# One accumulation of 512 columns instead of two of 256 in the input projection

## The chip, the cores and the metric

The kernel runs on one core of one Trainium2 chip. A core has five engines with an instruction queue each: TensorE (PE in the profile, with its weight loads as PEld), VectorE (DVE), ScalarE (ACT), GpSimd (POOL) and SyncE (SP, which here issues the DMAs). The metric is the device time of one execution in microseconds, median of three runs.

## The reference

Two layers of a mixer. Each layer modulates and normalises 256 context tokens and 2048 latent tokens of width 1024, multiplies them by one input projection, feeds a gated short convolution and a gated DeltaNet scan that runs in both directions, and multiplies the joined outputs by an output projection.

```python
pl = split_proj(to_scan_order(hl, col_major) @ w_in)
pc = split_proj(hc @ w_in)
dl = deltanet_inputs(pl[4], pl[5], pl[6], pl[8], pl[9], conv_qkv, a_log, dt_bias, seg_l)
dc = deltanet_inputs(pc[4], pc[5], pc[6], pc[8], pc[9], conv_qkv, a_log, dt_bias, seg_c)
ol, oc = bidirectional_gdn(dl, dc, ctx_out)
yl = from_scan_order(branch_outputs(pl, ol, conv_a, gdn_norm, seg_l), col_major)
xl = xl + gate_l * (yl @ w_out)
```

The scan solves a triangular system for every tile of tokens and then goes from tile to tile with a 128 by 128 state: `u = u0 - w s`, `s_new = s * decay + k u`.

## The kernel before

**Tokens and channels.** The 18 tiles of 128 tokens are cut into five chunks: chunk 0 is the context (256 tokens), chunks 1 to 4 are 512 latent tokens each. Activations lie channel-major in a high and a low part (`h` and `l`; `hc` and `lc` for the context). A unit is 128 output channels of `w_in`, whose weights are split in the same way (`whi`, `wlo`). `project` makes one unit of one chunk: 8 blocks of 128 input channels, three products each, so 24 passes over a chunk. `phase` walks over units and chunks and hands each result to a consumer (`conv`, tanh, multiply, store) that reads all columns of the accumulator at once.

**How many.** Per layer there are 32 units and four chunks of 512 tokens: 128 projections, 256 in both layers.

**The scan.** `delta` handles one head: for 16 tiles it transposes q, k, v (L495) and makes the k-k and q-k products (L511). Then comes one solve for all 16 tiles: multiplications and transposes on DVE (L543, L552), a transfer through DRAM that regroups blocks, a loop of 31 steps on DVE (L573, L575), a transfer back, and groups of small matmuls (L601, L610, L612, L630, L631, L637, L638) with DVE work between them (L582 to L640). Only then come the 32 scan steps of the head (two directions, 16 tiles). The chain of a step is L684 (PE), L686 (DVE), L689 (PE), L692 (DVE), L694 (PE), L703 (DVE), and then L684 of the next tile. L712 and L713 make the output of a step; `finish` turns finished tiles (L661, L662).

**The order.** The program is written with priorities (`urgent` raises them), and a list scheduler with a timeline of its own fixes the order of instructions on each engine when the kernel is built. Each engine then works its list strictly in that order. In layer 0 and layer 1 the scans of the four heads are emitted beside the last projections (`phase` with chunks 3 and 4 and later units), so small matmuls of the scan stand between projection matmuls. The output projection (L899, 512 columns) needs the finished tiles of all four heads.

Of the kernel before, what the change touches and what calls it, by code (L numbers as in the profile page):

```python
# [14 lines left out]
DRAM = bass.MemoryType.DRAM  # L15
# [14 lines left out]
CW = 256  # L30
# [6 lines left out]
def hybrid_backbone_kernel(ctx_stack: ExitStack, tc: tile.TileContext,  # L37
# [26 lines left out]
    turn = [0]  # L64

    def pidle():
        """The scan's banks in turn, for phases without a scan."""
        turn[0] += 1
        return pscan(("c0", "c1", "o")[turn[0] % 3])

# [32 lines left out]
            nc.vector.tensor_copy(csil[:, :, r:r + 1], ps[:, 8 * r:8 * r + 8].unsqueeze(2))  # L103

    def vectors(l, P):
        """Per-channel vectors of the layer, one column each."""
        rows = dp.tile([88, 128], F32, tag="dm", bufs=3, name="rows")
        nc.sync.dma_start(out=rows[0:24], in_=b_mod[l].rearrange("(k p) -> k p", p=128))
        nc.sync.dma_start(out=rows[24:32], in_=norm_w[l].rearrange("(k p) -> k p", p=128))
        nc.sync.dma_start(out=rows[32:44], in_=conv_a[l].rearrange("j (k p) -> (j k) p", p=128))  # L110
        nc.sync.dma_start(out=rows[44:80], in_=conv_qkv[l].rearrange("j (k p) -> (j k) p", p=128))
        nc.sync.dma_start(out=rows[80:81], in_=gdn_norm[l:l + 1])
        ps = pt()
        nc.tensor.transpose(ps[:, 0:81], rows[0:81], ident[0:81, 0:81])
        par = lp.tile([128, 88], F32, tag=f"par{l}", name="par")
        nc.vector.tensor_copy(par[:, 0:44], ps[:, 0:44])
        nc.vector.tensor_copy(par[:, 44:80], ps[:, 44:80])
        nc.vector.tensor_scalar(par[:, 32:44], par[:, 32:44], 0.5, None, ALU.mult)
        nc.vector.tensor_scalar(par[:, 80:81], ps[:, 80:81], 0.5, None, ALU.mult)
        P["par"] = par  # L120
        ab = lp.tile([128, 16], F32, tag=f"ab{l}", name="ab")
        nc.sync.dma_start(out=ab[:, 0:8], in_=a_log[l].rearrange("d h -> (d h)").partition_broadcast(128))
        nc.sync.dma_start(out=ab[:, 8:16], in_=dt_bias[l].rearrange("d h -> (d h)").partition_broadcast(128))
        nc.scalar.activation(ab[:, 0:8], ab[:, 0:8], AF.Exp)
        P["ab"] = ab
        P["mod"] = lp.tile([128, 24, 2], F32, tag=f"mod{l}", name="mod")
# [2 lines left out]
        nc.sync.dma_start(out=wm, in_=w_mod[l][:, 128 * j0:128 * j0 + 128 * n].rearrange("(k p) c -> p k c", p=128))  # L129

    def mod_piece(l, P, wm, j0, n, small):
        """Modulation of the n channel tiles from j0 on, for both kinds of tokens."""
        W = 128 * n
        acc = pd()
        for r in range(2):
            for q in range(4):
                k = 4 * r + q
                nc.tensor.matmul(acc[32 * q:32 * q + 32, 0:W], csil[:, k, :], wm[:, k, :], start=(r == 0), stop=(r == 1))
        acs = cp.tile([128, 512], F32, tag="y", bufs=YB, name="acs")
        nc.vector.tensor_copy(acs[:, 0:W], acc[:, 0:W])  # L140
        ps2 = small()
        for j in range(n):
            nc.tensor.matmul(ps2[:, 2 * j:2 * j + 2], acs[:, 128 * j:128 * j + 128], sel[:, 0:2], start=True, stop=True)
        nc.vector.tensor_tensor(P["mod"][:, j0:j0 + n, :], ps2[:, 0:2 * n].rearrange("p (j r) -> p j r", r=2),
                                P["par"][:, j0:j0 + n].unsqueeze(2).to_broadcast([128, n, 2]), ALU.add)
# [23 lines left out]
        nc.sync.dma_start(out=t, in_=cx[128 * g:128 * g + 128] if g < 2 else lat[128 * (g - 2):128 * (g - 2) + 128])  # L169

    def store_tokens(l, g, t):
        """Layer 0 writes its tokens in the scan order of layer 1, layer 1 in the order of the output."""
        if g < 2:
            nc.sync.dma_start(out=xc1[128 * g:128 * g + 128], in_=t)
            return
        n = GW if l == 0 else GR
        v = x1.rearrange("(w r) d -> r w d", r=GR) if l == 0 else out[0].rearrange("(r w) d -> w r d", w=GW)
        for q in range(128 // n):
            nc.sync.dma_start(out=v[(128 // n) * (g - 2) + q], in_=t[n * q:n * q + n])
# [12 lines left out]
        return dp.tile(shape, F32, tag="m2", bufs=4, name="hf")  # L192

    def prep_load(l, g0, n, tags):
        """Normalised tokens of the n tiles from g0 on. tags: the kinds of buffers they lie in, two tiles to each u but one to u.1."""
        xs = []
        for tag in tags:
            if tag[0] == "u":
# [14 lines left out]
        return xs  # L213

    def prep(P, xs, n, r, hi, lo, bank, bw, acc, keep):
        """Modulate n tiles of normalised tokens, channel-major, split them in two parts, and project on bw into acc. keep: where they are kept in DRAM."""
        for i in range(0, n, 2):
            o = slice(128 * i, 128 * i + 256)
            for k2 in range(0, KT, 2):
# [52 lines left out]
    def project(w, h):  # L272
        W = h[0].shape[-1]
        acc = pd()[:, 0:W]
        passes = [(k, i, j) for k in range(KT) for i, j in ((0, 0), (0, 1), (1, 0))]
        for c in range(0, W, CW):
            for z, (k, i, j) in enumerate(passes):
                nc.tensor.matmul(acc[:, c:c + CW], w[i][:, k, :], h[j][:, k, c:c + CW], start=(z == 0), stop=(z == len(passes) - 1))  # L278
        return acc

    def conv(dst, src, w, segs):
        """dst = segment convolution of src, w the three per-channel weights."""
        nc.scalar.activation(dst, src, AF.Identity, scale=w[1])
        n = dst.shape[-1]
        d3 = dst.rearrange("p (s t) -> p s t", t=segs)
# [2 lines left out]
        nc.vector.scalar_tensor_tensor(d3[:, :, 0:segs - 1], s3[:, :, 1:segs], w[2], d3[:, :, 0:segs - 1], ALU.mult, ALU.add)  # L288

    def layer(l, nxt):  # L290
        """Emits layer l; yields where the layer before it may go on. nxt: the layer after it."""
        ctx_out = l < LAYERS - 1
        seg_l = GW if l == 0 else GR
        P = {}
# [22 lines left out]
        bw = ba_weights()  # L317

        def logits(acc, ci, small, z_):
            """Sum the parts in acc: the write gate of the chunk, and its decay logits into z_."""  # L320
            g0, n = CHUNKS[ci]
            W = 128 * n
            part = stage([128, 512], n)
# [9 lines left out]
            return cp.tile([128, 8, 8], F32, tag=nm, bufs=1, name=nm)  # L333

        def gates(g0, n, z_, small):
            """Write gates and decays of the n tiles from g0 on."""
            gs = slice(g0, g0 + n)
            sm = lambda nm: small_tile(nm)[:, 0:n, :]
            bt = beta[:, gs, :]
# [36 lines left out]
            nc.sync.dma_start(out=row_d[8 * g0:8 * g0 + f8], in_=rw[0:f8])  # L376

        def qkv_unit(s, h):
            """s: 0 q, 1 k, 2 v."""
            par = P["par"]  # L380
            cw = [par[:, 44 + 12 * j + 4 * s + h:45 + 12 * j + 4 * s + h] for j in range(3)]

# [54 lines left out]
            return [unit(u) for u in (0, 2, 1, 3)]  # L437

        def phase(units, pairs, hs, after=None, again=False, ready={}):
            """units: (first column, consumer); the first and last two units go pair by pair."""  # L440
            N = len(units)
            tasks = []
            i = 0
# [30 lines left out]
        states = {}  # L474

        def delta(items, with_out, first):
            """items: (head, tile) pairs; each head's tiles are scanned both ways. Yields before the second eight."""
            n = len(items)
            U = []
            ssk = dp.tile([128, 16], F32, tag="ssk", bufs=2, name="ssk")  # L480
# [165 lines left out]
            og = {}  # L646

            def finish(h, i, o2):
                """Both directions are in o2: normalise two tiles, turn them channel-major."""
                g = items[i][1]  # L650
                tp = pscan("o")
                oT = dp.tile([128, 256], F32, tag="oT", bufs=1, name="oT")
# [97 lines left out]
        hs = {}  # L750

        def prep_pairs(ps, early={}, bank=pidle):
            """Operands and gates of the pairs ps."""
            g0, n = CHUNKS[ps[0]][0], sum(CHUNKS[p][1] for p in ps)
            with urgent():
                z_ = small_tile("g_z")
# [97 lines left out]
        mixes = [0]  # L854

        def mixed(g, aside):
            """Operands of tile g. aside: they leave the weights' buffers alone."""
            t0 = 128 * g
            ys = [dp.tile([128, 4, 128], F32, tag="m2", bufs=4, name="ys") for _ in range(2)]
            for i, yr in enumerate(ys):  # L860
# [96 lines left out]
```

## Time and profile before

| | |
|---|---|
| three runs | 2876.04, 2879.31, 2884.07 us |
| span of the profiled execution, first to last instruction | 2868.8 us |
| PE busy, share of the span | 96% |
| DVE busy | 63% |
| mean granted TensorE clock | 0.982 |

The profile gives the span of the profiled execution; its own time outside the span is not recorded apart, and the timed runs are 7.2 to 15.3 us longer than this span (the median 10.5 us). A busy PE is not a PE at its peak, because matmuls overlap: what counts is the distance from the start of one matmul to the start of the next.

### The profile page before, as it was taken

How to read it: one execution, taken by the hardware profiler on the slowest of the kernel's cores; microseconds unless marked ns; L12 is line 12 of the kernel's file. 1: busy time of each engine (PE TensorE's matmuls, PEld its weight loads, DVE VectorE, ACT ScalarE, POOL GpSimd, SP SyncE). 2: the span in 40 equal slices, each digit the busy share in tenths (PEclk: the TensorE clock that was granted, in tenths of full speed). 3: DMA queues.
4: the chain of work that ended last, by engine and by line, in shares of the span. 5: the costliest groups of instructions: out<-in, count | busy, mean ns of one | idle time of the engine just before them, and what ended most of it. 6: DMA issues, size and time to landing. Idle time of an engine off the chain costs nothing. (4 is left out here: it accounts for less than half of the span.)

```text
span 2868.8 us, 62580 instructions
## 1 busy us (share of the span) xinstructions
PE 2740.4 (96%) x23671; PEld 2529.1 (88%) x23671; DVE 1794.5 (63%) x4677; ACT 1139.6 (40%) x2962; POOL 1002.2 (35%) x1354
## 2 busy tenths in 40 slices
PE   7999999999999999999999999999999998999998
PEld 5799899988988999997777998899999888899887
DVE  5686657576586585353246776675766765754765
ACT  3544453533534532232115444435335354322332
POOL 2332322333433343234444222313334333333443
PEclk9999999999999999999999999999999999999999
DMA  8844265553655553347757552545546556434654
GB/s 275 251 120 138 81 174 130 174 162 89 182 145 170 173 139 113 109 149 246 239 161 242 162 144 79 154 112 163 154 115 188 132 168 189 126 116 118 206 173 117
DMA packets 589449, 450.17 MB, mean 157 GB/s; under 512 B 105322, under 2 KB 527196, under 8 KB 589148
## 3 DMA queue, kind: packets, MB, share of 16 engines
q1 hardware_dynamic: 589148, 446.16, 53.7%
q8 instruction: 188, 3.08, 0.4%
q14 instruction: 113, 0.93, 0.1%
HBM read 326.35 MB, written 119.70 MB: 155 GB/s over the span
## 5 line engine op out<-in xcount | busy, mean ns | idle before, releaser
L278 PE MATMUL pd<-h,whi 128*128 128x256 f32 x4096 | 1206.6, 295 | 2.1 <-ACT whi L251 2.1
L278 PE MATMUL pd<-l,whi 128*128 128x256 f32 x4096 | 1207.2, 295 | 0.0
L278 PE MATMUL pd<-h,wlo 128*128 128x256 f32 x4096 | 1199.4, 293 | 0.5 <-POOL wlo L253 0.5
L278 PEld LDWEIGHTS pd<-h,whi 128*128 128x128 f32 x4096 | 795.2, 194 | 11.9 <-issue 6.6
L278 PEld LDWEIGHTS pd<-l,whi 128*128 128x128 f32 x4096 | 795.0, 194 | 9.0 <-issue 5.4
L278 PEld LDWEIGHTS pd<-h,wlo 128*128 128x128 f32 x4096 | 794.8, 194 | 6.4 <-issue 2.9
L253 POOL TENSOR_TENSOR wlo<-raw,whi 128x1024 fp32r<-128x1024 f32 (+1 forms) x148 | 341.3, 2307 | 382.3 <-ACT whi L251 349.7
L899 PE MATMUL pd<-who,yy 128*128 128x512 f32 x1088 | 350.7, 397 | 0.4 <-ACT who L841 0.4
L899 PEld LDWEIGHTS pd<-who,yy 128*128 128x128 f32 x1088 | 203.6, 189 | 48.0 <-ACT yy L874 2.9
L697 ACT ACTIVATE w<-pscan,cs 128x128 f32<-128x128 f32 x272 | 99.5, 367 | 291.8 <-DVE wk L692 209.1
L899 PE MATMUL pd<-wlo,yy 128*128 128x512 f32 x544 | 214.1, 393 | 0.0
L251 ACT CAST whi<-raw 128x1024 fp32r<-128x1024 f32 x148 | 154.7, 1045 | 97.4 <-PE pd L278 60.9
L501 POOL TENSOR_TENSOR nk<-nk,phalf 128x1 f32<-128x1 f32 x144 | 81.7, 567 | 225.2 <-DVE nk L500 205.8
L573 DVE TENSOR_TENSOR tmp<-L,X 64x31 f32<-64x31 f32 (+15 forms) x310 | 127.1, 410 | 39.9 <-DMA L<-blk 25.0
L388 ACT ACTIVATE pd<-y 128x512 f32<-128x512 f32 (+1 forms) x116 | 65.5, 565 | 213.0 <-DVE y L288 200.6
L686 DVE SCALAR_TENSOR_TENSOR r<-pscan,eg,rc 128x128 f32<-128x128 f32 x272 | 93.7, 346 | 76.7 <-PE pscan L684 74.5
L575 DVE TENSOR_TENSOR X<-X,tmp 64x31 f32<-64x31 f32 (+15 forms) x310 | 136.3, 440 | 5.6
L692 DVE TENSOR_SCALAR wk<-pscan,cs 128x128 f32<-128x128 f32 x272 | 93.5, 346 | 69.6 <-PE pscan L689 67.7
L875 POOL TENSOR_TENSOR yy<-ys,yy 128x512 fp32r<-128x512 f32 x68 | 89.9, 1323 | 125.4 <-ACT yy L874 118.3
L660 POOL TENSOR_TENSOR so<-so,mhalf 128x1 f32<-128x1 f32 x136 | 79.2, 590 | 142.5 <-DVE so L659 134.3
L703 DVE SCALAR_TENSOR_TENSOR Sn<-Sn,atot,pscan 128x128 f32<-128x128 f32 x240 | 82.0, 342 | 67.9 <-PE pscan L694 66.6
L874 ACT CAST yy<-ys 128x512 fp32r<-128x512 f32 x68 | 42.1, 619 | 198.2 <-DVE ys L867 136.8
(2212 smaller groups left out, 5317.3 us busy)
## 6 DMA issues: line engine op xcount, KB each, us to landing
raw<-in_w_in_dram SPq DMA_DIRECT2D x148, 512.0 KB, 4.8
rc<-rec_d SPq DMA_DIRECT2D x272, 256.0 KB, 3.1
rec<-rec_d SPq DMA_DIRECT2D x136, 192.0 KB, 2.6
wm<-in_w_mod_dram SPq DMA_DIRECT2D x24, 1024.0 KB, 7.3
rec_d<-y SPq DMA_DIRECT2D x96, 256.0 KB, 2.9
rows<-row_d SPq DMA_DIRECT2D x144, 128.0 KB, 4.1
rec_d<-rec SPq DMA_DIRECT2D x144, 128.0 KB, 4.0
ys<-y_d SPq DMA_DIRECT2D x68, 256.0 KB, 3.5
```

The costliest lines, as they stand in the source:

```text
L251: nc.scalar.copy(hi, raw)
L253: eng.tensor_sub(lo[:, k], raw[:, k], hi[:, k].bitcast(F32))
L278: nc.tensor.matmul(acc[:, c:c + CW], w[i][:, k, :], h[j][:, k, c:c + CW], start=(z == 0), stop=(z == len(passes) - 1))
L501: nc.gpsimd.tensor_tensor(nk[:, i:i + 1], nk[:, i:i + 1], phalf[:, 0:1], ALU.pow)
L573: nc.vector.tensor_tensor(t3, L3[:, j + 1:32, j:j + 1].to_broadcast([2 * nb, m, k]), X3[:, j:j + 1, 0:k].to_broadcast([2 * nb, m, k]), ALU ...
L575: nc.vector.tensor_sub(X3[:, j + 1:32, 0:k], X3[:, j + 1:32, 0:k], t3)
L686: nc.vector.scalar_tensor_tensor(r, p1[:, 0:128], eg[:, g, col], vn, ALU.mult, ALU.subtract)
L692: nc.vector.tensor_scalar(wk, p2[:, 0:128], cs[:, 5 + z0 + d, i:i + 1], None, ALU.mult)
L697: nc.scalar.activation(w, p2[:, 0:128], AF.Copy, scale=cs[:, z0 + d, i:i + 1])
L703: nc.vector.scalar_tensor_tensor(Sn, S, atot[:, g, col], p3[:, 0:128], ALU.mult, ALU.add)
L875: nc.gpsimd.tensor_sub(l_, yr, h_.bitcast(F32))
L899: nc.tensor.matmul(acc, yy[k // 4][:, k % 4, :], wo[k][part][:, cs_], start=(z == 0), stop=(z == 23))
```

## The change

`project` loses the loop over halves of 256 columns. A chunk of 512 tokens is now accumulated in 24 matmuls of 512 columns; before, it took 48 of 256 columns, first all 24 for the left half, then all 24 for the right half. Columns and products are the same; every weight block is loaded once where it was loaded twice. The context chunk (256 columns) stays as it was.

```diff
         acc = pd()[:, 0:W]
         passes = [(k, i, j) for k in range(KT) for i, j in ((0, 0), (0, 1), (1, 0))]
-        for c in range(0, W, CW):
-            for z, (k, i, j) in enumerate(passes):
-                nc.tensor.matmul(acc[:, c:c + CW], w[i][:, k, :], h[j][:, k, c:c + CW], start=(z == 0), stop=(z == len(passes) - 1))
+        for z, (k, i, j) in enumerate(passes):
+            nc.tensor.matmul(acc, w[i][:, k, :], h[j][:, k, :], start=(z == 0), stop=(z == len(passes) - 1))
         return acc
```

Behind that line the changed file is one line shorter: L277 is L278 of before, L683 is L684, and so on. The text below uses the numbers of before.

The scheduler makes a new order from this. In the built programs the projection has 13,248 matmuls before (12,288 on chunks of 512 tokens) and 7,104 after (6,144 of 512 columns). All other matmuls are the same 6,457. What stands on PE at the end of each layer, for its last head, counted in the order:

| on PE, last head | layer 0 before | layer 0 after | layer 1 before | layer 1 after |
|---|---|---|---|---|
| projections from the last L511 to the first L601 | 434 of 256 | 301 of 512 | 423 of 256 | none |
| matmuls of the scan (L684 to L713) in the same stretch | 60 | 58 | 57 | 97 |
| projections from the first L601 to the last L638 | 111 of 256 | none | 107 of 256 | none |
| L899 in the same stretch | none | 24 | none | 24 |
| projections from there to the closed row of L899 | 1246 of 256 | none | 954 of 256 | none |
| matmuls of the scan in the same stretch | 165 | 134 | 126 | 109 |

Two places on PE show it. First, layer 1 right behind the last L511 of the last head, before (`pt` is a small bank of the accumulator memory, `pd` the one of the projection, `pscan` one of the scan):

```order
L511 MATMUL pt<-rec 128x256
L278 MATMUL pd<-l,whi 128x256
L278 MATMUL pd<-h,wlo 128x256
L278 MATMUL pd<-h,whi 128x256
L278 MATMUL pd<-l,whi 128x256
L278 MATMUL pd<-h,wlo 128x256
```

and the same place after the change, where the next instructions are those of the scan of the head before:

```order
L510 MATMUL pt<-rec 128x256
L693 MATMUL pscan<-wk,rc 128x128
L712 MATMUL pscan<-w,P__24272 128x128
L693 MATMUL pscan<-wk,rc 128x128
L683 MATMUL pscan<-Sn,rc 128x128 x2
L711 MATMUL pscan<-Sn,rc 128x128
L712 MATMUL pscan<-w,P__24298 128x128
L688 MATMUL pscan<-r,V__24308 128x128
L688 MATMUL pscan<-r,V__24334 128x128
```

Behind the L511 the projections are gone; steps of the two directions follow each other. The second place is layer 1 behind the last matmul of the last solve, before:

```order
L638 MATMUL pt<-v_29957,zq 64x64
L278 MATMUL pd<-h,whi 128x256
L278 MATMUL pd<-l,whi 128x256
L278 MATMUL pd<-h,wlo 128x256
L694 MATMUL pscan<-wk,rc 128x128
L278 MATMUL pd<-h,whi 128x256
```

and after, where the first scan steps of the last head begin:

```order
L637 MATMUL pt<-v_25733,zq 64x64
L688 MATMUL pscan<-r,V__26015 128x128
L688 MATMUL pscan<-r,V__26041 128x128
L693 MATMUL pscan<-wk,rc 128x128
L712 MATMUL pscan<-w,P__26031 128x128
L693 MATMUL pscan<-wk,rc 128x128
L683 MATMUL pscan<-Sn,rc 128x128
L711 MATMUL pscan<-S_26011,rc 128x128
L712 MATMUL pscan<-w,P__26057 128x128
```

Here too no projection is left to stand between one link of the chain and the next.

## Rows read from the trace of the kernel before

**Rows 1.** Page, part 1: busy time, share and instructions of each engine.

```profile
PE 2740.4 (96%) x23671; PEld 2529.1 (88%) x23671; DVE 1794.5 (63%) x4677; ACT 1139.6 (40%) x2962; POOL 1002.2 (35%) x1354
```

**Rows 2.** Waits of PE: who was waited for; us in total, times, longest us.

```profile
PE pt L601 <- DMA tf<-blk: 14.2, 6, 3.4
PE pscan L684 <- DVE Sn L703: 14.0, 15, 2.8
PE pscan L689 <- DVE r L686: 11.4, 9, 3.3
```

**Rows 3.** Chain that ended last: start us, us, engine, tile, line, count.

```profile
2528.64 2.27 PE pd L278 x19
...
2548.48 2.88 PE pd L278 x24
...
2767.19 5.69 PE pd L899 x25
...
2787.00 62.38 PE pd L899 x275
```

**Rows 4.** Cores: span and mean granted clock.

```profile
core 0: 2868.8 us, clock 0.982
```

**Rows 5.** Timeline of PE, a scan step between projections: start us, us, instruction.

```profile
2540.67 0.28 PE L278 MATMUL pd<-h,wlo 128*128 128x256 f32 x1
2540.79 0.38 PE L689 MATMUL pscan<-r,V__29017 128*128 128x128 f32 x2
2540.93 0.37 PE L278 MATMUL pd<-h,whi 128*128 128x256 f32 x1
2541.13 0.28 PE L278 MATMUL pd<-l,whi 128*128 128x256 f32 x1
```

**Rows 6.** Timelines of PE and DVE: bounds of the last solve of layer 1.

```profile
2413.33 0.59 PE L511 MATMUL pt<-rec 128*128 128x256 f32 x2
...
2487.30 0.25 PE L601 MATMUL pt<-tf,U 32*32 32x32 f32 x4 [1.88 <-DMA tf<-blk]
...
2525.42 0.69 DVE L640 TENSOR_SCALAR U<-pt 64x512 f32<-64x512 f32 x1
```

**Rows 7.** Windows, L278 on PE alone: length, busy (count), clock, DMA share, GB/s.

```profile
2414.00:2487.30 73.30, 60.51 (x423) 0.98 0.49 122
```

**Rows 8.** Windows, all engines: length, busy of PE, PEld, DVE, ACT, POOL, clock.

```profile
2414.00:2487.30 73.30, 66.51 (x541) 65.35 (x539) 56.66 (x166) 18.94 (x45) 29.12 (x47) 0.98 0.49 122
2487.30:2526.10 38.80, 38.58 (x645) 34.51 (x646) 29.97 (x77) 18.16 (x41) 11.16 (x19) 0.96 0.45 131
```

**Rows 9.** DVE groups, 2413.9 to 2487.3: busy us, mean ns, idle before, releaser.

```profile
L573 DVE TENSOR_TENSOR tmp<-L,X 128x31 f32<-128x31 f32 (+15 forms) x31 | 12.6, 408 | 6.3 <-DMA L<-blk 5.8
...
L692 DVE TENSOR_SCALAR wk<-pscan,cs 128x128 f32<-128x128 f32 x12 | 4.1, 344 | 2.8 <-PE pscan L689 2.8
...
L287 DVE SCALAR_TENSOR_TENSOR xa<-cx,par,xa 128x496 f32<-128x496 f32 x2 | 1.5, 750 | 0.6 <-ACT xa L283 0.6
...
L582 DVE STREAM_TRANSPOSE vf<-tf 128x512 f32<-128x512 f32 x1 | 0.7, 711 | 4.3 <-DMA tf<-blk 4.3
```

**Rows 10.** Timelines: one link of the scan's chain without a queue in it.

```profile
333.59 0.39 PE L684 MATMUL pscan<-Sn,rc 128*128 128x128 f32 x2
...
334.01 0.35 DVE L686 SCALAR_TENSOR_TENSOR r<-pscan,eg,rc 128x128 f32<-128x128 f32 x1 [0.26 <-PE pscan L684]
...
334.51 0.38 PE L689 MATMUL pscan<-r,V__2091 128*128 128x128 f32 x2
```

**Rows 11.** Timelines: the small matmuls of the context's solve in layer 0.

```profile
229.31 0.32 PE L601 MATMUL pt<-tf,U 32*32 32x32 f32 x4 [3.23 <-DMA tf<-blk]
...
249.43 0.69 DVE L640 TENSOR_SCALAR U<-pt 64x512 f32<-64x512 f32 x1
```

**Rows 12.** Page, parts 5 and 6: what lies between a finished tile and L899.

```profile
L875 POOL TENSOR_TENSOR yy<-ys,yy 128x512 fp32r<-128x512 f32 x68 | 89.9, 1323 | 125.4 <-ACT yy L874 118.3
...
ys<-y_d SPq DMA_DIRECT2D x68, 256.0 KB, 3.5
```

## The prediction

> **What bounds the kernel now.** I read the busy shares first: PE is busy for 96% of the span, DVE for 63% [rows 1]. A busy PE says little by itself, so the waits of PE come next. They are few and short: the solve's transfer costs 14.2 us in 6 waits, the two most frequent links of the scan 14.0 and 11.4 us [rows 2]. So PE always has something to do, and the time of the kernel is the sum of distances between matmul starts. These distances are best read in the chain that ended last, where long rows are pure streams: 24 projection matmuls of 256 columns take 2.88 us, 0.1200 each, and 275 matmuls of 512 columns in the output projection take 62.38 us, 0.2268 each [rows 3]. Two halves cost 0.2400, one full width costs 0.2268. The timeline shows why PE has no gaps: a scan matmul is slipped into the stream of projections. From 2540.67 to 2541.13 are 0.46 us for two projections and one L689, so the scan matmul costs 0.22 [rows 5], and the 0.9 us until its answer is back [rows 10] pass under projections. The reader should see in this that projections have two jobs: they are the bulk of the work, and they are the cover for everything that has to wait.
>
> **What the change removes.** 6,144 pairs become single matmuls. At 0.2400 - 0.2268 = 0.0132 us a pair that is 81 us. The least favourable rows of the same chain (19 in 2.27 us, so 0.1195; 25 in 5.69 us, so 0.2276) give 0.0114 and 70 us [rows 3]. The mean granted clock is 0.982 [rows 4], so with levels of 1.0 and 0.5 some 3.6% of the time lies at the lower one, where I count no gain: 81 x 0.964 = 78 us. I take 78, bounds 70 and 81.
>
> Both widths show the same surplus over columns at 2.4 GHz: 0.120 - 0.1067 and 0.2268 - 0.2133, 13.4 ns each [rows 3], so it is a cost per matmul. The Trainium skill, "TensorE: Matmul & The Clock Gate", section "Back-to-back issue gap", gives columns over 2.4 GHz plus about 2.5 ns for a matmul by itself. By that the change would be worth only 6,144 x 2.5 ns = 15 us. The rows above disagree with it for these float32 operands with a weight load each, and I go by the rows.
>
> **What the change moves.** The other effect lies in the order. Scan matmuls stand in fewer places between projections than before, the scan gets along more slowly per column of projection, and when the projections of a layer are used up, its last head is not done. The table of the change shows it: in layer 1 no projection is left behind the last L511, in layer 0 none behind the first L601. What was covered there lies open.
>
> Layer 1, from the last L511 to the first L601. Before, this takes 73.3 us (2414.0 to 2487.3), with 423 projections in it [rows 6, 7] and PE idle for 73.3 - 66.5 = 6.8 [rows 8]. Of PE's work, 423 x 0.120 = 51 us leave, and 40 more scan matmuls come in at 0.22 (9 us): 73 - 7 - 51 + 9 = 24 us of work are left. How long does the stretch last now? It is a chain through DVE and two transfers. DVE works 56.7 us in it before [rows 8]. The consumers of two projections leave (five groups like L287, 1.4 to 1.5 us each, 7 us), and 8 more scan steps come in, each three links of 0.34 and outputs of nearly the same size, 2 us: 57 - 7 + 16 = 66 us. While the transfers are under way DVE stood idle for 5.8 and 4.3 us [rows 9]. That makes 76; I take 80 because a link that is late now holds up DVE's list (2.8 us already before, at L692 [rows 9]). Loss: 80 - 24 - 7 = 49 us. Bounds: 35 (66 us, everything else hidden) and 59 (73 + 16 = 89, the old length with the extra steps on top).
>
> Layer 1, from there to the last DVE operation of the solve. Before, 38.8 us, PE busy for 38.6 [rows 8]. Without the projections and 21 scan matmuls, with 24 L899, PE needs at most 24 us, and less as the small matmuls were waiting behind projections; I estimate 19. The context's solve, of half the size, goes through it in 250.1 - 229.3 = 21 us [rows 11]. I take 28, loss 9; bounds 0 (24 and 24) and 15 (39 and 24).
>
> Layer 1, the first half of the last head's scan. 109 scan matmuls at 0.22 and some others are 26 us of PE. Two directions of about 12 steps run side by side, each step three links. A link without a queue takes 334.51 - 333.59 = 0.92 us [rows 10]; with one matmul of the other direction ahead of it 1.14. So a step takes 2.8 to 3.4, with DVE's other work up to 3.6; I take 3.1: 37 us, loss 11, bounds 7 and 17. Then the first finished tile has to go out to DRAM and back (3.5 us each way) and through GpSimd (1.3 us for a half) before L899 can use it [rows 12]; some 10 us, part of it under scan steps: 6, bounds 0 and 12.
>
> Layer 0 keeps 301 projections of 512 columns (68 us) between L511 and L601, so nothing is lost there. From L601 on it is as in layer 1: 7 for the small matmuls (0 to 15), 13.5 steps x 3.1 = 42 against 134 x 0.22 and some others, 32: 10 (5 to 17), and 6 (0 to 12) for the way to L899.
>
> Something comes back too: links under projections get longer pauses, so of the 25 us that PE waits at L684 and L689 [rows 2] I take 6 off (0 to 25).
>
> **Sum.** Losses 49 + 9 + 11 + 6 + 7 + 10 + 6 - 6 = 92 us, gain 78: the profiled execution goes from a span of 2868.8 [rows 4] to 2883. The median of the runs shown is 10.5 us above that span, so I forecast 2893 us. The lowest bounds of the losses add up to 35 + 7 + 5 - 25 = 22, the highest to 59 + 15 + 17 + 12 + 15 + 17 + 12 = 147.
>
> **The rivals.**
>
> Faster, because the open stretches are short. With no projection consumers on DVE, ScalarE and GpSimd the solve runs near its bare length, 66 us and not 80, the small matmuls cost nothing extra, and the waits of rows 2 vanish. For it: DVE was busy with other things in the solve. Against it: the two transfers are waits that nothing shortens. With losses of 45 the time is 2879 - 78 + 45 = 2846. It decides where losses fall under 69 us.
>
> Slower still, because DVE's list is worked strictly in order and the scan of the head before now stands densely between the steps of the solve: each late link delays the solve, and the solve delays the link. With losses of 130 the time is 2931. For it speaks that DVE idles behind links already with cover [rows 9]; against it that the two chains can fill each other's waits.
>
> The cover isn't missed: the scan on the chip runs ahead, so that nothing lies open, and the kernel gains all 78 us: 2801. Against it stands that PE works its list in order, and the list has no projections there.
>
> The pace doesn't change: a projection matmul of 512 columns, with its operands, takes twice 0.12. Then only the losses are left: 2971. L899 with the same kind of operands speaks against it [rows 3]. The rule of the Trainium skill on the page named above would lead near this case, with 15 us of gain.
>
> **How the numbers follow.** A measurement of this kernel can tell about 0.3% (8.6 us) from no change: 2870.7 to 2887.9 is the same. I give the forecast case 0.46, with its own range of 2878 to 2911 (losses of 77 to 110); the short stretches 0.22 (2830 to 2878); the dear ones 0.20 (2911 to 2956); no open stretch 0.07; no change of pace 0.05. Of the forecast case about a third lies within 0.3%, 0.15, and 0.02 of the short stretches. Faster: 0.20 + 0.07 = 0.27. Same: 0.17. Slower: 0.31 + 0.20 + 0.05 = 0.56. The range of 2835 to 2950 leaves out the two last cases (0.12) and 0.03 at either end of the middle ones.
>
> **What would show it.** In the profile after: streams of L277 at 0.227 us a matmul in the chain; two new lows of PE's busy share, one at the end of each layer's projections, and layer 1's the deeper; between the last L510 and the first L600 of the run some 80 us with hardly 25 us of PE work, the waits of PE there put down to DVE's L575 or to transfers of `tf`; waits at L683, L688 and L693 of the order of 1 us, tens of them in a row. The granted clock should fall in the first of these stretches, which costs little as no projection stands in it. The forecast is wrong if the solve of the last head takes less than 60 us without cover, or if PE waits more than before elsewhere too, because the new order fits the chip less well in places that I didn't work out.

## The result

The changed kernel takes 2963.21 us (median, 2959.9 to 2967.81), the kernel before beside it 2877.68: ratio 1.0296, 95% interval 1.028 to 1.0313. It is slower, as forecast, but by 85.5 us where 14 were forecast, and 13 us above the range.

The page of the changed kernel: its busy shares, then PE and the granted clock in 40 slices. Below it, the same two rows of the kernel before.

```profile
PE 2770.6 (94%) x17527; PEld 2243.1 (76%) x17527; DVE 1798.3 (61%) x4677; ACT 1139.5 (38%) x2962; POOL 999.0 (34%) x1354
...
PE   7999999999999999779999989989999989978898
...
PEclk7999999999999999689999999999999999966899
```

```profile
PE   7999999999999999999999999999999998999998
...
PEclk9999999999999999999999999999999999999999
```

Two lows, at the end of each layer's projections, and at both of them the granted clock falls too; before, the clock row held nothing but nines. The forecast had layer 1's low as the deeper one; in PE's row it is not. The mean clock is 0.945 [rows 4: 0.982]. The streams of projections came out at the forecast pace, in the chain that ended last:

```profile
2226.97 4.58 PE pd L277 x20
...
2521.64 4.81 PE pd L277 x21
```

0.229 us each, against 0.120 for half the columns [rows 3]; over the whole trace, the median from the start of one such matmul to the next is 0.227. The next view is a table of eight windows: the last head's solve (from its last L510 to its first L600), its small matmuls, the first half of its scan, and the way to the 48th L898, for layer 0 and then for layer 1. Columns: window, length, busy time and instructions of PE, PEld, DVE, ACT and POOL, granted clock, DMA share, GB/s.

```profile
1109.70:1191.20 81.50, 75.84 (x423) 64.97 (x423) 65.87 (x192) 27.79 (x58) 31.23 (x49) 0.95 0.55 154
1191.20:1230.50 39.30, 33.78 (x528) 26.30 (x530) 21.38 (x68) 15.25 (x39) 7.95 (x18) 0.67 0.48 140
1230.50:1290.70 60.20, 45.49 (x240) 36.59 (x237) 32.50 (x119) 16.18 (x56) 16.52 (x51) 0.77 0.47 144
1290.70:1319.70 29.00, 20.50 (x81) 15.75 (x80) 13.51 (x44) 6.04 (x20) 10.40 (x19) 0.71 0.53 154
2607.00:2683.50 76.50, 56.31 (x210) 43.58 (x209) 58.33 (x236) 21.96 (x72) 26.08 (x65) 0.58 0.52 139
2683.50:2713.10 29.60, 24.34 (x492) 19.42 (x494) 15.12 (x43) 12.60 (x28) 4.22 (x8) 0.64 0.29 90
2713.10:2748.70 35.60, 29.39 (x175) 24.57 (x172) 21.42 (x69) 12.33 (x34) 10.14 (x36) 0.86 0.58 164
2748.70:2776.70 28.00, 20.56 (x81) 15.97 (x80) 13.37 (x45) 6.18 (x21) 10.03 (x19) 0.70 0.55 161
```

Layer 0 of the kernel before in the same four windows:

```profile
999.90:1069.30 69.40, 66.69 (x560) 66.08 (x558) 60.20 (x187) 20.00 (x52) 31.06 (x49) 1.00 0.50 132
1069.30:1104.50 35.20, 34.14 (x622) 30.13 (x621) 23.38 (x71) 16.70 (x40) 8.40 (x18) 1.00 0.43 124
1104.50:1218.70 114.20, 114.20 (x974) 114.13 (x971) 49.70 (x131) 29.64 (x73) 34.88 (x59) 1.00 0.38 111
1218.70:1305.10 86.40, 85.64 (x681) 83.19 (x680) 50.15 (x131) 28.69 (x68) 36.53 (x49) 1.00 0.54 168
```

Before, PE fills the windows, most of it with projections, at full clock. After, the windows of the bare scan are shorter, but they hold no projection at all. To see what that costs I priced PE's work in every window (projections and output matmuls as in [rows 3], a scan matmul 0.22 as in [rows 5], small ones 0.05, an estimate) and took it from the window's length. What is left is lost time. Lost time after, less lost time before, beside the losses of the prediction (us):

| stretch | layer 0: predicted | measured | layer 1: predicted | measured |
|---|---|---|---|---|
| solve of the last head | 0 | 8 | 49 | 44 |
| its small matmuls | 7 | 12 | 9 | 6 |
| first half of its scan | 10 | 35 | 11 | 17 |
| way to L898, and the output projection behind it | 6 | 19 | 6 | 11 |
| sum | 23 | 74 | 75 | 78 |

Everywhere else: -6 predicted, +23 measured. Of these 17 lie in layer 1 between the last L510 of the context and that of the first head, and 14 between those of its second and of its third head. In layer 0, from the last L510 of the first head to that of the last, where projections of 512 columns stand beside three scans, lost time is 8 us less than before; in layer 1 the same stretch loses 15 more, the 14 among them. So 152 of the 175 us lie where the last head has lost all or part of its cover, and what wide matmuls cost beside a covered scan is in the 23. PE's priced work shrank by 82 us (78 predicted). 74 + 78 + 23 - 82 = 93, the distance between the two last L898. In layer 1 the sum is right; in layer 0 and in the rest it is not.

The medians lie only 85.5 us apart. Every timed run on record is 1.7 us or a little more above its span, so the span of 2868.8 stands for an execution of some 2870.5 us, 7 us quicker than the kernel's median. About 7 of the 93 us are therefore no effect of the change.

PE's waits, the longest sums:

```profile
PE pscan L693 <- ACT w L696: 29.7, 39, 3.3
PE pscan L683 <- DVE Sn L702: 18.6, 20, 3.8
PE pscan L688 <- DVE r L685: 11.3, 19, 1.9
...
PE pscan L661 <- DVE o L660: 10.4, 8, 3.0
```

Before, the longest sum was another, which [rows 2] leaves out:

```profile
PE pt L495 <- DMA rec<-rec_d: 20.0, 17, 3.6
```

The scan's links are now what PE waits for most, and the largest of them, 29.7 us in 39 waits, is p3 (the matmul of L693) behind ACT's reading of p2 (the result of L688); both use the same bank.

### The profile page after: what moved, and what is told of

It reads as the page before. It is cut to its first block, busy times and chain, and to the rows that moved or that the text cites. A ratio compares the mean times of both kernels' runs of the same rounds, so it can differ in the third digit from the quotient of the medians.

```text
span 2961.5 us, 50270 instructions
## 1 busy us (share of the span) xinstructions
PE 2770.6 (94%) x17527; PEld 2243.1 (76%) x17527; DVE 1798.3 (61%) x4677; ACT 1139.5 (38%) x2962; POOL 999.0 (34%) x1354
## 5 line engine op out<-in xcount | busy, mean ns | idle before, releaser
L277 PE MATMUL pd<-h,whi 128*128 128x512 f32 x2048 | 832.6, 407 | 20.5 <-DVE y L388 5.8
L277 PE MATMUL pd<-h,wlo 128*128 128x512 f32 x2048 | 831.0, 406 | 5.6 <-POOL wlo L253 5.6
L277 PE MATMUL pd<-l,whi 128*128 128x512 f32 x2048 | 829.1, 405 | 0.5 <-DVE l L253 0.5
L277 PEld LDWEIGHTS pd<-h,whi 128*128 128x128 f32 x2048 | 390.9, 191 | 102.4 <-DVE y L388 8.6
L277 PEld LDWEIGHTS pd<-h,wlo 128*128 128x128 f32 x2048 | 390.8, 191 | 84.2 <-POOL wlo L253 7.8
L277 PEld LDWEIGHTS pd<-l,whi 128*128 128x128 f32 x2048 | 391.1, 191 | 76.3 <-issue 2.1
L898 PE MATMUL pd<-who,yy 128*128 128x512 f32 x1088 | 356.4, 403 | 1.4 <-ACT yy L873 1.4
L898 PEld LDWEIGHTS pd<-who,yy 128*128 128x128 f32 x1088 | 205.6, 191 | 48.5 <-ACT yy L873 3.3
L898 PE MATMUL pd<-wlo,yy 128*128 128x512 f32 x544 | 218.5, 402 | 0.0
L693 PE MATMUL pscan<-wk,rc 128*128 128x128 f32 x544 | 125.3, 316 | 32.7 <-ACT w L696 29.7
L693 PEld LDWEIGHTS pscan<-wk,rc 128*128 128x128 f32 x544 | 98.7, 210 | 55.9 <-ACT w L696 43.1
L683 PE MATMUL pscan<-Sn,rc 128*128 128x128 f32 x512 | 117.1, 317 | 22.1 <-DVE Sn L702 18.6
L574 DVE TENSOR_TENSOR X<-X,tmp 64x31 f32<-64x31 f32 (+15 forms) x310 | 125.2, 404 | 6.4
```

The costliest lines, as they stand in the source:

```text
L277: nc.tensor.matmul(acc, w[i][:, k, :], h[j][:, k, :], start=(z == 0), stop=(z == len(passes) - 1))
L574: nc.vector.tensor_sub(X3[:, j + 1:32, 0:k], X3[:, j + 1:32, 0:k], t3)
L683: nc.tensor.matmul(p1[:, 0:128], kT, S, start=True, stop=True)
L693: nc.tensor.matmul(p3[:, 0:128], kn, wk, start=True, stop=True)
L898: nc.tensor.matmul(acc, yy[k // 4][:, k % 4, :], wo[k][part][:, cs_], start=(z == 0), stop=(z == 23))
```

## The experiments

The theory from here on, the cover theory: the scan of the heads is one long chain; projections are its cover, and it moves by one link whenever the list lets it. A stretch of the scan with no projection in it is called bare. With 512 columns more time passes between two links. The list itself shows that: among the scan matmuls of heads 0 to 3 of layer 0 stand 103, 118, 118 and 135 us of projections before, and 154, 161, 111 and 0 after. So the cover is gone before the last head comes. Rivals: wide matmuls slow what runs beside them, wherever they stand; the bare stretches are slow through the clock; new orders differ by chance.

**256 beside the scans (e1).** 512 columns in the phases of q, k, v; 256 in the last two phases.

```diff
-    def project(w, h):
+    def project(w, h, cw=512):
...
+        for c in range(0, W, cw):
...
-        phase(units, (3, 4), hs, late)
+        phase(units, (3, 4), hs, late, cw=CW)
-        phase(units, cl, hs, again=True)
+        phase(units, cl, hs, again=True, cw=CW)
```

> 512 column matmuls everywhere but in the two last projection phases of each layer, beside which the scans of heads 0 to 3 run; there two accumulations of 256 as before. The cover theory (the loss is the cover that runs out, because one wide matmul in place of two narrow ones takes more time at each place of the list where a scan matmul waits its turn): in the list 15 and 41 scan matmuls of the 374 of a layer stand behind the last projection (before 4 and 26, changed kernel 128 and 163), projections shrink by 30 us a layer, so 2878 - 60 + 10 to 20 = about 2832 (2820 to 2850). If 512 wide matmuls themselves slow what runs beside them, wherever they stand, 60/159 of the projections' gain and of the loss would be there: about 2905. If the loss had nothing to do with the scans' cover, 2878 - 60 + 92 = about 2910.

Measured: 2879.53 us, ratio 0.9985 (0.9966 to 1.0004). The loss is gone, far from both rivals (2905 and 2910), but the gain isn't there either. One number of the expectation was wrong: 1,152 pairs a layer at 0.0132 us are 15 us, not 30, so that it should have read 2858 to 2868. The trace shows where the gain went, in two places. Layer 1 begins 15.6 us earlier than before, but behind the last product of its first head it is 12 us late. The stretch from the context's last L510 (of the changed kernel's numbers) to that of the first head takes 252 us in e1 and 239 before, with 3 us less of PE's work in it. First window the changed kernel, then e1, then before:

```profile
1649.30:1901.90 252.60, 236.87 (x1288) 183.23 (x1287) 162.71 (x376) 109.38 (x264) 67.90 (x72) 0.96 0.42 119
1608.60:1860.90 252.30, 235.13 (x1287) 181.96 (x1286) 163.54 (x376) 109.29 (x264) 67.89 (x72) 0.97 0.42 119
1610.20:1848.90 238.70, 231.41 (x1981) 214.82 (x1980) 163.47 (x376) 108.88 (x262) 65.12 (x71) 0.98 0.45 124
```

It is 250 to 253 us in all six runs with 512 columns there and the banks of before (the changed kernel, e1, e2, e3, e10, e12), and 237 to 242 in those with 256 and all the work (before, e4, e8, e11). So wide matmuls, or the order that comes with them, do cost some 10 us in this one place, and cover doesn't explain it. The second place is the end of layer 1: projections run out early, and the window from the second half of the last head's scan to the 48th L900 (L899 of before) has PE busy for 27.7 of 37.3 us, where before it was busy for 40.6 of 40.6. The window of e1, then that of before:

```profile
2654.60:2691.90 37.30, 27.70 (x120) 21.97 (x119) 19.42 (x52) 11.03 (x26) 12.39 (x21) 0.77 0.60 191
2637.60:2678.20 40.60, 40.60 (x301) 38.45 (x300) 27.22 (x55) 15.79 (x31) 18.66 (x23) 1.00 0.59 188
```

**Cheaper projections without any change of width (e9).** The question that e1 raised: what is a saved microsecond of projections worth in this kernel? This kernel leaves out one product of each accumulation.

```diff
-        passes = [(k, i, j) for k in range(KT) for i, j in ((0, 0), (0, 1), (1, 0))]
+        passes = [(k, i, j) for k in range(KT) for i, j in ((0, 0), (0, 1), (1, 0))][:-1]
```

> The kernel before, widths of 256, with the last of the 24 matmuls of each projection accumulation left out (the product of one low part, k = 7, is missing from the output). Projections shrink by 66 us (552 accumulations of one matmul at 0.120), nearly what the wide matmuls save, but the scan's matmuls keep their distance in the list (head by head 101, 126, 114, 105 and 119, 123, 116, 67 us of projections among them; before 103, 118, 118, 135 and 112, 114, 120, 99). If the time is the sum of PE's work, 2878 - 66 = 2812. If the scan's chain through the heads has slack in layer 0 (some 45 us there, since the last head's first half ends 73 us before the output projection) and none in layer 1, the gain of layer 0 alone is seen: 2845 (2830 to 2855). If the chain sets the end of both layers: 2870 or above. Orders by chance move it by up to 15 us.

Measured: 2841.19 us, ratio 0.9887 (0.9865 to 0.9908): 33 of 66 us. In the trace, where the two profiled executions lie 24 us apart, the split differs from the expected one: layer 1 starts 16 us earlier, and adds 7. In layer 1 the last projection starts 48 us earlier than before and the last L899 only 24, and here too the stretch in front of the output projection lies open (19.3 of 25.5 us busy, clock 0.78):

```profile
2634.30:2659.80 25.50, 19.30 (x83) 15.12 (x83) 13.03 (x46) 6.51 (x21) 10.38 (x20) 0.78 0.57 164
```

So projections and scan were near balance before, and half of this saving was lost although most links kept their distance. A new order can move the time by some 15 us (e8, below), so the half is a rough figure.

**Half the dose (e12).** 512 everywhere, but 256 in the last phase of each layer.

```diff
-        phase(units, cl, hs, again=True)
+        phase(units, cl, hs, again=True, cw=CW)
```

> 512 columns everywhere but in the last projection phase of each layer, which keeps 256. Half the dose: by the list 74 and 23 us of projections are left behind the first small matmul of head 3 (changed kernel 0 and 0, before 163 and 127), 63 and 97 scan matmuls stand bare (128 and 163; 4 and 26). Cover theory: projections 56 us shorter, half of the 175 us lost: 2878 - 56 + 90 = 2912 (2895 to 2930), between e1 and the changed kernel. If width beside the first heads' scans were what costs, whatever cover is left at the end, 2940 or above.

Measured: 2901.67 us, ratio 1.0093 (1.0072 to 1.0114), inside the cover theory's interval and far below the rival's 2940. With e1 and the changed kernel it makes a row of doses: by the list 140 and 103, 74 and 23, 0 and 0 us of projections are left behind the first small matmul of the last head in the two layers, and the ratios are 0.9985, 1.0093 and 1.0296. The same runs also have more and more wide matmuls beside the scans; that these are not the main cost is shown by the table of the result, where 152 of the 175 us lie in the last head's stretches and 23 everywhere else.

**Layer 0 alone (e4).**

```diff
-                a = project(w[j], hs[p])
+                a = project(w[j], hs[p], 512 if l == 0 else CW)
```

> 512 column matmuls in layer 0 only. Cover theory: layer 1 starts 25 us later than before, as in the changed kernel, and then runs like before: 2878 + 25 = 2903 (2890 to 2915); layer 1 of the changed kernel carries the other 60 us. If the loss came in layer 1 whatever layer 0 does, about 2795.

Measured: 2925.98 us, ratio 1.0132 (1.0104 to 1.016), 11 us above the interval. But the kernel before took 2885.62 us beside it, and the expectation counted from 2878; by the ratio the time is 2916, at the interval's edge. In the trace layer 1 starts 31 us late, near the expected 25, and with the widths of before loses 24 more until its end, spread over its whole length. The two profiled executions lie 55 us apart, the medians taken beside each other 40, so some 15 of the 55 us come from the quick execution that was profiled of the kernel before. How much of the 24 is left stays open, and cover doesn't explain it.

**A new list and nothing else (e8).**

```diff
                 gates(g0, n, z_[:, 0:n, :], bank)
+                if ps == (1, 2):
+                    nc.tensor.matmul(bank()[:, 0:16], ident, ident[:, 0:16], start=True, stop=True)
```

> The kernel before with one matmul of 16 columns per layer that nobody reads, behind the gates of chunks 1 and 2. No work to speak of is added (0.2 us), but the list comes out anew: 98, 124, 114, 139 us of projections among the scan matmuls of heads 0 to 3 of layer 0 where before has 103, 118, 118, 135. It measures what a new order alone is worth in the places nobody worked out: if orders are as good as each other, 2878 within 5; if a list's places matter by chance as the run with layer 0 alone hints (layer 1 lost 20 us there with the widths of before), 10 to 25 us either way.

Measured: 2886.36 us, ratio 1.0054 (1.0036 to 1.0071): 15 us slower (10 to 20) for two matmuls of 16 columns. In the trace nothing is lost right behind the first of them: at the last L511 of layer 0's first head this run is 1.5 us ahead of before, and falls back later. Any edit of this kernel makes the list anew, and this one new list cost 15 us. The 23 us elsewhere in the result are of this size, but their largest part, in layer 1 before its first head, came back in all six runs with 512 columns there and the banks of before. Whether the width or the order that comes with it is at fault is not shown: no run here changes the widths and keeps the list.

**Another way to denser links (e5, e6, e7).** The kernel has eight accumulator buffers in PSUM, called banks here: three for projections, two for transposes, three for the scan. These runs give the scan's outputs a second one and leave the projections two. e5 is the changed kernel with that, e6 the kernel before, and e7 has 512 columns in layer 0 and in layer 1's phases of q, k, v.

```diff
-    psd = pool("psd", 3, space=PSUM)
+    psd = pool("psd", 2, space=PSUM)
...
-        return pss.tile([128, 512], F32, tag=tag, name="pscan")
+        return pss.tile([128, 512], F32, tag=tag, bufs=2 if tag == "o" else 1, name="pscan")
```

> The changed kernel with two PSUM banks for the scan's outputs (tag o) in place of one, taken from the projections' accumulators (two in place of three). The list alone says: in layer 0 now 140 us of projections are left behind the first small matmul of head 3 (changed kernel 0, before 163) and 35 scan matmuls stand behind the last projection (128, 4); in layer 1 still 0 and 137 (changed 0 and 163, before 127 and 26). Cover theory: layer 0's loss of about 74 us shrinks to 10 to 20, layer 1's 78 to about 65: 2963 - 70 = about 2893 (2875 to 2915). If the loss isn't made by missing cover but by the wide matmuls beside the scan, no more than 20 us come back: 2940 or above. Two accumulators may cost PE waits: 0 to 30 us on top of either.

> The kernel before with the same exchange of banks: two for the scan's outputs, two for the projections. By the list 220 and 148 us of projections are left behind the first small matmul of head 3 and no scan matmul stands bare. Cover theory: before already lost little in its two ends (some 10 to 25 us against full cover), so 2878 - 10 to -25, plus 0 to 30 for the missing accumulator: about 2875 (2850 to 2905). The pair e5 and e6 differ in the width alone: cover theory expects their difference at +20 us (0 to 40) where the pair with one bank differs by 85; the theory that wide matmuls slow the scan expects +70 or more again.

> Two banks for the scan's outputs, 512 columns in all of layer 0, in layer 1 only in the phases of q, k and v; 256 in layer 1's last two phases. List: 140 and 132 us left behind the first small matmul of head 3, 35 and 4 bare. Projections are 56 us shorter than before. Cover theory: 2878 - 56 + 10 to 20 in layer 0 + 0 to 30 for the accumulator: 2845 (2825 to 2875), faster than both kernels. If pre-scan phases give nothing whatever the cover (as the run with 256 beside the scans might be read), 2870 or above.

Measured: e5 2933.11 us, ratio 1.0213 (1.0191 to 1.0235); e6 2937.76, 1.0234 (1.0216 to 1.0253); e7 2902.9, 1.0118 (1.0092 to 1.0143). e6 and e7 lie above their intervals; e5 lies near the rival's bound and by itself decides nothing. The two accumulators cost far more than I allowed: e6 loses 67 us with nothing bare, and its longest wait is a new one, projections behind the consumer of an older accumulator. e5 has it too. First e6, then e5:

```profile
PE pd L278 <- DVE y L389: 25.1, 21, 4.3
```

```profile
PE pd L277 <- DVE y L388: 32.2, 23, 4.3
```

So e7 beats the changed kernel but not the one before. The pair speaks against the rival all the same. At equal banks the width now makes a difference of -5 us (e5 less e6), where it made +85 with one output bank; the expectation was 0 to 40, and 70 for the rival. That the missing accumulator costs both widths alike is assumed, not shown. In e5 layer 0's list has its cover back, and the window of the last head's first half is full again, at full clock:

```profile
1137.70:1272.00 134.30, 134.30 (x777) 117.68 (x778) 54.31 (x135) 35.85 (x80) 40.01 (x61) 1.00 0.35 105
```

Which of the two exchanged banks made the list denser was not taken apart on the chip.

**The clock (e2, e3, e10).** Matmuls that nobody reads, added to the changed kernel for the last head of each layer alone (`hot`), while the solve runs, between its small matmuls, and (not in e10) in each step of its scan. e3 has the same instructions with 16 columns.

```diff
+        def warm(rhs, c, to=None):
+            nc.tensor.matmul(pt()[:, 0:c] if to is None else to, ident, rhs, start=True, stop=True)
...
+                if hot and j >= (16 if l else 22):
+                    warm(X[:, 32 * j + 32:32 * j + 64].unsqueeze(1).to_broadcast([128, 16, 32]), 512)
...
+                if with_out and not first and h == NH - 1:
+                    warm(kT[:, 0:128], 128, p2[:, 256:256 + 128])
```

> The changed kernel plus matmuls that nobody reads, for the last head of each layer alone: 512 columns after the last steps of the triangular solve (9 in layer 0, 15 in layer 1), six behind it, two between its small matmuls, and 128 columns in each step of its scan; the list keeps its order. The clock theory (about 50 us of the loss is TensorE at 1.2 GHz in the bare stretches): the clock stays at 2.4 GHz there, the small matmuls and scan steps shrink by 40 to 50 us, the added matmuls cost 5 to 15: about 2925 (2910 to 2940). The rival (bare stretches are slow for VectorE, GpSimd or transfers, and the clock is only a sign of it): 2963 or slower by the added work, 2965 to 2985.

> Control for the run with added matmuls: as many instructions at the same places, each of 16 columns. Clock theory: the clock still falls, and time is that of the changed kernel or up to 10 us more (2960 to 2975). If it were the added instructions that shift waits and not the clock, this run would gain as much as the one with 512 and 128 columns.

> As the run with wide added matmuls, but without those of the scan's steps: 512 columns after the last steps of the solve, six behind it, two between its small matmuls, for the last head of each layer. Clock theory: the small matmuls and the first rounds of the bare scan run at 2.4 GHz, and the 14 us that the added matmuls of the steps cost are gone: 2940 (2930 to 2952) against 2963 of the changed kernel. If the clock in the solve doesn't carry into the scan behind it, 2952 to 2960; if the added matmuls cost what they give, 2963.

Measured: e2 2958.07 us (ratio 1.0253, 1.022 to 1.0286), e3 2981.1 (1.0328, 1.0301 to 1.0355), e10 2955.85 (1.0287, 1.0267 to 1.0306). The kernel before took 2885.62 us beside e2 and e3, so the ratios are the better measure against the changed kernel's 1.0296. e2's expectation was 2910 to 2940, so 40 to 50 us net aren't to be had: by the ratio some 12 are left. e3 came out 6 us over its interval, and by the ratio inside it. But with equal instructions 23 us lie between e2 and e3. The windows show it best: in layer 0 of e3 the first half of the bare scan is worked at 1.2 GHz (granted clock 0.50), in e2 at 2.4 GHz (0.99). First two windows of e3 (the whole stretch, then a part of it), then two of e2:

```profile
1227.20:1309.30 82.10, 69.49 (x284) 59.40 (x285) 36.03 (x129) 17.45 (x60) 18.40 (x56) 0.56 0.38 114
1264.00:1303.00 39.00, 35.53 (x147) 31.99 (x147) 15.09 (x49) 7.51 (x24) 7.08 (x24) 0.50 0.35 102
```

```profile
1236.30:1290.80 54.50, 43.52 (x259) 36.04 (x256) 31.46 (x110) 15.87 (x53) 16.10 (x50) 0.84 0.53 153
1264.00:1290.80 26.80, 23.22 (x167) 20.42 (x167) 17.09 (x54) 8.73 (x27) 8.07 (x28) 0.99 0.63 172
```

82.1 us against 54.5 for the same stretch. One step, from L725 to the next L725 (the other direction's) in the timeline of e3, takes 3.22 us, so a round, one step in each direction, takes 6.4 with its two added matmuls. PE is busy for 35.5 of 39 us there, so little but PE's own pace is left to bound the scan:

```profile
1266.84 0.77 PE L725 MATMUL pscan<-Sn,rc 128*128 128x128 f32 x2
...
1270.06 0.77 PE L725 MATMUL pscan<-Sn,rc 128*128 128x128 f32 x2
...
1273.28 0.77 PE L725 MATMUL pscan<-Sn,rc 128*128 128x128 f32 x2
```

In e10 the small matmuls are at 2.4 GHz in both layers (1.00, before the added work 0.67 and 0.64) and take 29.4 and 25.0 us instead of 39.3 and 29.6:

```profile
1202.40:1231.80 29.40, 29.37 (x549) 23.16 (x548) 20.64 (x69) 12.25 (x32) 8.81 (x22) 1.00 0.47 151
1231.80:1285.40 53.60, 44.03 (x224) 34.88 (x219) 30.92 (x111) 15.86 (x53) 15.96 (x50) 0.75 0.51 154
2670.60:2695.60 25.00, 21.87 (x510) 16.95 (x509) 14.23 (x43) 10.25 (x25) 5.49 (x11) 1.00 0.31 105
```

In the scan behind them the clock falls again, to 0.75 in layer 0, and the solve in front is 8 us longer for the added work, so that hardly anything is left: the ratio of 1.0287 can't be told from the changed kernel's 1.0296. The clock in the solve doesn't carry over, as the second line of the expectation had it.

**A kernel that beats both (e11).** 512 only where a wide matmul meets no head's scan and where there is slack: layer 0, phases of q, k, v.

```diff
-                a = project(w[j], hs[p])
+                a = project(w[j], hs[p], cw if l == 0 else CW)
```

> 512 columns only in layer 0 and only in its phases of q, k and v; everything else 256 as before. A candidate that may beat both kernels: layer 0 with these widths ended 15 us earlier in the run with 256 beside the scans, layer 1 is as before. If layer 0's lead lasts: 2863 (2855 to 2870). If layer 1 comes out differently because its list is made anew: up to 20 us on top, 2863 to 2885.

Measured: 2863.07 us, ratio 0.997 (0.9956 to 0.9984), as expected for a lead that lasts. It is faster than both kernels, by 9 us against the one before. It keeps layer 1 narrow, and so has not the slow stretch that e1 has there (240 us, not 252). But one list can be worth 15 us more than another (e8), so that the gain isn't shown to come from the widths.

## Why the prediction missed

**Right.** The pace (0.229 in the chain against 0.227), the places of the loss, and in layer 1 the solve without cover (76.5 us where 80 were said) and the small matmuls (29.6, 28 said). The gain of 78 is borne out as far as the pace is: PE's work shrank by 82 us if each wide matmul is priced at the 0.2268 of [rows 3], and by 68 at 0.229. The sentence that projections are cover as well as bulk is what the windows and e12 bear out. The Trainium skill, "TensorE: Matmul & The Clock Gate", section "Back-to-back issue gap", gives 2.5 ns for a matmul by itself, by which I estimated a gain of 15 us. The distances in these streams, 0.227 against twice 0.120, make it 80, so that figure is not the one for them.

**Right by luck.** The first half of the last head's scan in layer 1 took 35.6 us, where 37 were said. But the 37 were for 12 rounds at 3.1 us, up to the 48th L898. The window of 35.6 us holds 84 scan matmuls, which is 8.4 rounds, at 4.2 us each, and 28 us more pass until the 48th L898.

**Wrong.** The step that failed is the price of the last head's bare scan: 3.1 us a round in both layers, with "From L601 on it is as in layer 1" for layer 0 (10 us of loss for 13.5 rounds, 35 measured), and the way to L898 (6 us, 19 measured). Eleven rounds fill the 60.2 us of layer 0's first half, and at 3.1 they would take 34. One L711 stands in each step, so two in each round:

```profile
1231.06 0.39 PE L711 MATMUL pscan<-Sn,rc 128*128 128x128 f32 x2
...
1257.07 0.80 PE L711 MATMUL pscan<-S,rc 128*128 128x128 f32 x2
...
1265.18 0.63 PE L711 MATMUL pscan<-Sn,rc 128*128 128x128 f32 x2
1267.98 0.40 PE L711 MATMUL pscan<-Sn,rc 128*128 128x128 f32 x2
1269.86 0.39 PE L711 MATMUL pscan<-Sn,rc 128*128 128x128 f32 x2
...
1290.47 0.39 PE L711 MATMUL pscan<-Sn,rc 128*128 128x128 f32 x2
```

First, all steps were priced alike. Those before 1257 are second-half steps of head 2, with L661 and the normalisation: three rounds fill the 26.6 us from 1230.5 to the first L711 of head 3, where 9.3 were allowed. Layer 1 has none of them in its window.

Second, "The granted clock should fall in the first of these stretches, which costs little as no projection stands in it." It fell in layer 0 too (0.67, 0.77 and 0.71 in three windows), and further on than the first stretch in both, and there the scan's own matmuls stand in it. The scan of head 3 shows both levels, 1.2 GHz (granted clock 0.50) until 1268 and 2.4 GHz behind it:

```profile
1257.70:1268.00 10.30, 8.72 (x36) 7.54 (x36) 3.88 (x13) 2.50 (x8) 1.76 (x6) 0.50 0.44 125
1268.00:1290.70 22.70, 17.20 (x124) 14.91 (x124) 14.00 (x49) 7.49 (x24) 7.02 (x24) 1.00 0.58 170
```

Until 1267.98 a step takes 2.8 us, behind it 1.88: a round costs 5.6 us at 1.2 GHz and 3.75 at 2.4 (3.45 in layer 1). Two rounds at 1.2 GHz take 10.9 us where 6.2 were allowed. Six at 2.4 GHz take 22.5 where 18.6 were allowed, so that the price was low at full clock too. Part of head 2's rounds is at 1.2 GHz as well, but how much of their length is the clock's is not shown: the first of them took 9.8 us at 2.4 GHz. In the small matmuls of layer 0 I estimate the clock's part at 10 us (39.3 less e10's 29.4).

Third, the way to L898 was counted as one trip through DRAM under some cover. The chain of the changed kernel shows two trips and two rounds of the second half, in layer 1:

```profile
2748.05 2.15 DMA o_d<-o
2750.22 2.42 DMA o<-o_d
...
2753.59 0.80 PE pscan L711 x2
...
2761.44 2.53 DMA y_d<-oT
2764.03 3.08 DMA ys<-y_d
...
2769.20 2.56 PE pd L898 x6
```

21 us, with no projection under any of it. Before, the second half of the last head started 73 us ahead of the output projection in layer 0 and hid it all.

Two smaller things. The solve of layer 0, put at nothing, lost 8 us. The table of the change has 301 projections of 512 columns there, and the prediction 68 us of cover; but 109 of the 301 belong to the context chunk and have 256 columns, so the cover is 57 us. And the PE work of layer 1's small matmuls, "at most 24 us", comes to 26.6 by its own rows, which changed little.

The term of -6 for links that get longer pauses came out as +23. The waits at L684 and L689, 14.0 and 11.4 us [rows 2], did not vanish (L683 and L688: 18.6 and 11.3), and those at L693 came on top. This is the prediction's own second sign of being wrong, more waits in places that it didn't work out; the largest, before layer 1's first head, goes with 512 columns there. Of the rivals, the unchanged pace came nearest in time (2971), by luck, as the pace did change. "DVE's list strictly in order", with losses of 130, came nearest to the losses (175), but for a reason it didn't give: the solve of layer 1 was not longer than forecast.

**Left open.** What the clock cost in all: 23 us (e2 against e3) is what one pair showed, for added work that itself costs something. It is no measure of the changed kernel, whose clock rose again at 1268 with nothing added, while e3's stayed at 0.50 until 1303 at least. And whether the +23 comes from the width itself or from the orders that came with it.

## What to carry to other kernels

Before a matmul is made larger in a list that interleaves two chains, count in the list what the other chain gets: here each matmul became 1.89 times as long, and the cover that one head uses up went from 103 to 154 us. Where bulk work and a chain are near balance, a saving in the bulk can be worth half of itself (e9: 33 of 66 us) or less than nothing (the changed kernel). Price bare stretches by each kind of step for itself, at both clocks, and with each trip through DRAM on the way out. And compare times taken beside each other: the kernel before had medians from 2871 to 2886 us on different occasions.

## What was not expected of the hardware

A PE that is busy by the profile can stay slow. In 39 us of e3's bare scan the granted clock was 0.50 throughout, with PE busy for 35.5 of them and added matmuls of 16 columns in each step; with 128 columns in the same places the stretch was granted 0.99, and with no added matmuls the changed kernel's clock rose in the same scan, from 0.50 to 1.00 at 1268. And two matmuls of 16 columns that no one reads moved a kernel of 2871 us by 15 us, most likely by the order alone.
